# A two-layer hybrid trunk: the triangular inverses of layer 0's delta rule taken two heads at a time, with a new order of projection tiles

## The chip, the cores and the metric

One core of one Trainium2 chip runs the whole program: two layers of a sequence model on 512 tokens (256 latent, 256 context), all weights streamed from HBM. The metric is the time of one execution in microseconds. Before the change it is 1524.98 us, the median of three runs (1524.62 to 1525.18).

## The reference, cut to what matters

Each layer normalizes and modulates its input, projects it once (w_in), runs three branches on column groups of the projection, gates each branch by its own SiLU path, and projects back (w_out) with a gated residual. The change touches one branch, the gated delta rule of four heads, in two directions, in chunks:

```python
strict = jnp.tril(jnp.einsum('bhnid,bhnjd->bhnij', kb, k) * decay, -1)
eye = jnp.eye(cs, dtype=jnp.float32)
t_mat = lax.linalg.triangular_solve(eye + strict, jnp.broadcast_to(eye, strict.shape),
                                    left_side=True, lower=True, unit_diagonal=True)
u = t_mat @ (v * beta[..., None])
w = t_mat @ (kb * jnp.exp(g)[..., None])
...
def step(s, inp):
    q_i, k_i, u_i, w_i, qk_i, gl_i = inp
    v_new = u_i - w_i @ s
    o = q_i @ s + qk_i @ v_new
    s = s * jnp.exp(gl_i)[..., None, None] + jnp.swapaxes(k_i, -1, -2) @ v_new
    return s, o
```

A is `strict`, the strictly triangular matrix of a chunk; its inverse with ones on the diagonal is `t_mat`. The other branches are a linear recurrence (RG-LRU) of four column groups and an attention of eight heads.

## The kernel before

**Tiles and quarters.** A layer's activations lie transposed as 16 blocks of 128 features, each split in a high and a low part, `xh[k]` and `xl[k]`, in a 32-bit format that TensorE multiplies in one pass. A projection tile is 128 output columns; `accumulate` (L399) makes it from three matmuls for each k (`wh` with `xh`, `wl` with `xh`, `wh` with `xl`), 48 in all, into the PSUM tile `pz`. `project` (L405) goes through a tile in four quarters of four k; each quarter needs one pair `wh`, `wl` of 512 columns, which ScalarE (`wh`, a cast) and VectorE (`wl`, the difference) make from the raw weights in `split_w` (L356). There are four such pairs, and `Weights.ahead` (L385) keeps three made ahead. The first seven tiles of layer 0 (`FIRST`, L23) are made during its start; then come 37 tiles in the order of the table `ORDER` (L24) and 16 tiles of w_out. The 37 tiles are called the body here and counted 0 to 36, with quarters as fractions.

**What each tile sets off.** The table's names say whose columns a tile holds: gk, gv, gq are keys, values and queries of a delta-rule head; kc, vc, qc attention; xa the RG-LRU; ga, gb, gc the gates. `consume` (L1097) hands a finished tile to a generator: `gdn_k`, `gdn_v`, `gdn_q`, `attn_...`, `rglru`. `gdn_q` (L750) adds `gdn_head` (L761), one generator for a whole head, to lane 0 of the class `Background` (L470); attention and RG-LRU go to lane 1. Between pairs of k, `between` (L1124) calls `pump`, which issues the next step of each lane whose earlier step should be done by the clocks that `Timed` (L51) keeps while the program is written; where VectorE should be idle it also issues a piece of layer 1's modulation, 512-column multiply-adds into `macc` on VectorE. The build's scheduler then fixes each engine's order. So TensorE's queue is the stream of `pz` matmuls with short stretches of other work between them, and each engine works off its queue in order.

**A head.** `gdn_head` makes the products of k with k and q (`kk`), the decay matrices in two `wa` tiles, and A in a third `wa` tile (`a2`, L785). `invert(a2)` (L872) inverts both directions at once, by blocks: on the diagonal 32x32 blocks four levels of two products (`small`, L897: 16 matmuls of 32x32 each, at 16 places of the array), each followed by work on VectorE (a masked product into `ym`, tile `s`; or an addition and a 32x32 transpose, tiles `tt` and `ti`, both of the tag `c`); then two more such products, and three of 64x64 (`large`, L928: 8 matmuls). That is 13 dependent products a head. The result goes into the tile `full`, of which there is one, and which POOL first clears (L880). Then the head's scan reads it.

**The RG-LRU** (`rglru_scan`, L959) works in a tile `th`, of which there is one. **The end of the body:** after the last tile `bg.drain()` (L1164) issues what is left, and `split_x` (L338) splits the 16 blocks Y of the branches' outputs into `xh[k]` (ScalarE) and `xl[k]` (VectorE) for w_out, whose first tile reads them in the order of k.

Of the kernel before, what the change touches and what calls it, by code (L numbers as in the profile page):

```python
# [13 lines left out]
P = 128  # L14
KT = 16
T = 256
# [8 lines left out]
    "vc0 kc0 gc4 qc0 qc1 gk1 gv1 qc2 gq1 gk2 qc3 gv2 gq2 kc1 vc1 qc4 qc5 gk3 gv3 gc6 qc6 qc7 gb0 gq3 xa0 xa1 gc5 ga2 xa2 gb1 gb2 xa3 gb3 ga0 ga1 ga3 gc7",  # L25
# [69 lines left out]
def trunk(ctx, tc, xT, cT, consts, masks, rope_t, small, fg, w_mod0, w_mod, w_first, w_in, w_ba, w_rg, w_out, out):  # L95
# [121 lines left out]
    class Narrow:  # L217
# [390 lines left out]
    def layer(l, acc, bs):  # L608
# [152 lines left out]
        def gdn_head(h, rq):  # L761
            kq, kt, vt = gd[h]["kq"], gd[h]["kt"], gd[h]["vt"]

            bb = tmp("bb", (P, 2, 4, 2))
            for x, name in enumerate(("beta", "bt")):
                dve.tensor_tensor(out=bb[:, x], in0=gate[name].rearrange("p c (d h) -> p c d h", d=2)[:, :, :, h],
                                  in1=gd[h]["r2"][:, 0:4].unsqueeze(2).to_broadcast([P, 4, 2]), op=ALU.mult)
            kk = [pa_() for _ in range(2)]
            for c in range(4):
                w = 2 * P if c < ncq else P  # L770
                pe.matmul(out=kk[c // 2][:, 256 * (c % 2):256 * (c % 2) + w], lhsT=kq[:, c, 0, :],
                          rhs=kq[:, c].rearrange("p x t -> p (x t)")[:, 0:w], start=True, stop=True)
            kkv = [k_.rearrange("p (c x t) -> p c x t", c=2, x=2) for k_ in kk]
            qkds, dts = [], []
            for d in range(2):
                j = 4 * d + h

                dt_ = tmp("wa")
                nc.sync.dma_start(out=c3(dt_), in_=gate["rd"][:, j, :].partition_broadcast(P))
                pool.tensor_tensor(out=c3(dt_), in0=c3(dt_), in1=maskb[d].unsqueeze(1).to_broadcast([P, 4, P]), op=ALU.add)  # L780
                for c in range(4):
                    act.activation(out=dt_[:, c * P:c * P + P], in_=dt_[:, c * P:c * P + P], func=AF.Exp, bias=gate["ncum"][:, c, j:j + 1])
                dts.append(dt_)
                yield
            a2 = tmp("wa")  # L785
            for c in range(4):
                cc = slice(c * P, c * P + P)
                dve.tensor_scalar(out=a2[:, cc], in0=dts[0][:, cc], scalar1=bb[:, 0, c, 0:1], scalar2=None, op0=ALU.mult)
                dve.scalar_tensor_tensor(out=a2[:, cc], in0=dts[1][:, cc], scalar=bb[:, 0, c, 1:2], in1=a2[:, cc], op0=ALU.mult, op1=ALU.add)
            for x in range(2):  # L790
                dve.tensor_tensor(out=c3(a2[:, 256 * x:], 2), in0=c3(a2[:, 256 * x:], 2), in1=kkv[x][:, :, 0, :], op=ALU.mult)
            yield
            for d in range(2):
                qkd = dts[d]
                for x in range(2):
                    if 2 * x < ncq:
                        dve.tensor_tensor(out=c3(qkd[:, 256 * x:], 2), in0=kkv[x][:, :, 1, :], in1=c3(dts[d][:, 256 * x:], 2), op=ALU.mult)
                qkds.append(qkd)
            yield
            tts = yield from invert(a2)  # L800
# [71 lines left out]
        def invert(a2):  # L872
            rows = [slice(32 * i, 32 * i + 32) for i in range(4)]
            tt = tmp("c", (P, 2, 4, 32))
            ti = tmp("c", (P, 2, 4, 32))
            ac = tmp("s", (P, 4, 32))
            full = tmp("full", (P, 2, TT), bufs=1)
            fv = full.rearrange("p d (c t) -> p d c t", t=P)
            av = c3(a2)
            pool.memset(full, 0.0)  # L880
            for i in range(4):
                (act.copy if i % 2 else dve.tensor_copy)(ac[rows[i]], av[rows[i], :, rows[i]])
            yield
# [401 lines left out]
```

## Time and profile before

| | |
|---|---|
| median of three runs | 1524.98 us |
| the profiled execution | 1525.27 us, span 1523.4 us |
| TensorE (PE) busy | 1466.0 us, 96% of the span |
| VectorE (DVE) busy | 1165.2 us, 76% |
| ScalarE (ACT) busy | 739.3 us, 49% |
| GpSimd (POOL) busy | 110.8 us, 7% |
| layer 0's start | 0 to 143 us |
| layer 0's body, 37 tiles | 143.1 to 731.7 us |
| layer 0's w_out, 16 tiles | 731.7 to about 911 us |
| layer 1 | from about 911 us on |

A matmul's time in a row is from its start to its end, and the next begins before that end; so the time that it costs is read from start to start. In rows of matmuls of plain 32-bit floats the trace has two records for each matmul: "pa<-c,s x32" is one `small` product of 16.

### The profile page before, as it was taken

To read this page: it belongs to the slowest core of one execution; us is meant where nothing else is said; L and a number is where in the kernel's file an instruction comes from. 1 tells how busy PE (TensorE), PEld (TensorE's weight loads), DVE (VectorE), ACT (ScalarE), POOL (GpSimd) and SP (SyncE) were. 2 spreads that over 40 slices of the span, in tenths; PEclk is the share of its full clock that TensorE was granted. 3 is DMA by queue.
4 is the path that set the end of the run, shared out by engine and by line. 5 is a ranking of instruction groups with operands and counts; after the bars stand their busy time and mean duration, and the time that the engine had idled before them with its cause. 6 is when DMAs were issued, how large, how long until landed. Compare 5 with 4: busy or idle time off the path is not lost.

```text
span 1523.4 us, 30014 instructions
## 1 busy us (share of the span) xinstructions
PE 1466.0 (96%) x11762; PEld 1210.7 (79%) x11762; DVE 1165.2 (76%) x2513; ACT 739.3 (49%) x1708; POOL 110.8 (7%) x114
## 2 busy tenths in 40 slices
PE   4999999999999999999999999999999999999996
PEld 3777778777877877788888877778878899779996
DVE  5446898989898798999657877777885776778754
ACT  4324435545444546654422225444544555777653
POOL 0000100100100100000011110010100101000011
PEclk9999999999999999999999999999999999999998
DMA  9994544434443452445346655645542333224653
GB/s 358 396 387 158 163 137 131 145 112 145 154 139 126 129 180 91 132 136 175 125 142 210 217 189 193 186 157 164 190 150 74 98 117 112 71 91 138 192 183 111
DMA packets 87310, 247.68 MB, mean 163 GB/s; under 512 B 9280, under 2 KB 20992, under 8 KB 87168
## 3 DMA queue, kind: packets, MB, share of 16 engines
q1 hardware_dynamic: 86016, 244.71, 48.9%
q8 instruction: 92, 1.51, 0.4%
q10 hardware_dynamic: 1152, 1.05, 0.2%
q14 instruction: 50, 0.41, 0.1%
HBM read 243.60 MB, written 2.13 MB: 161 GB/s over the span
## 4 chain that ended last, share of the span: by engine, by line
PE 76%; DVE 10%; issue 7%; ACT 3%; DMA 2%; POOL 1%; SPq 0%; DVEq 0%; POOLq 0%; ACTq 0%
PE pz L89 55%; PE pa L89 8%; PE pb L89 8%; PE pt L89 3%; PE pm L89 3%; DVE wb L89 2%; DMA wraw<-in_w_in 2%; DVE wl L89 1%; DVE macc L89 1%; DVE th L89 1%; DVE o L89 1%; ACT t L89 1%; ACT wb L89 1%; DVE Y L89 1%; DVE wa L89 1%
## 5 line engine op out<-in xcount | busy, mean ns | idle before, releaser
L89 PE MATMUL pz<-xh,wh 128*128 128x512 f32 (+1 forms) x1760 | 643.8, 366 | 1.8 <-ACT xh L89 1.8
L89 PE MATMUL pz<-xh,wl 128*128 128x512 f32 (+1 forms) x1760 | 629.8, 358 | 0.8 <-DVE wl L89 0.8
L89 PE MATMUL pz<-xl,wh 128*128 128x512 f32 (+1 forms) x1760 | 628.2, 357 | 0.0
L89 ACT CAST wh<-wraw 128x512 fp32r<-128x512 f32 x488 | 294.2, 612 | 339.5 <-PE pz L89 203.3
L89 DVE TENSOR_TENSOR wl<-wraw,wh 128x512 fp32r<-128x512 f32 x488 | 327.6, 679 | 139.4 <-ACT wh L89 137.8
L89 PEld LDWEIGHTS pz<-xl,wh 128*128 128x128 f32 x1760 | 332.1, 189 | 49.4 <-DVE xl L89 0.6
L89 PEld LDWEIGHTS pz<-xh,wh 128*128 128x128 f32 x1760 | 332.1, 189 | 47.5 <-ACT xh L89 1.9
L89 PEld LDWEIGHTS pz<-xh,wl 128*128 128x128 f32 x1760 | 332.7, 189 | 42.7 <-DVE wl L89 1.5
L89 DVE SCALAR_TENSOR_TENSOR macc<-wm,cs,macc 128x512 f32<-128x512 f32 x400 | 293.5, 765 | 1.1 <-DMA wm<-in_w_mod 0.5
L89 PE MATMUL pb<-wb 128*128 128x128 f32 (+1 forms) x560 | 113.4, 330 | 3.9 <-ACT wb L89 2.0
L89 PEld LDWEIGHTS pb<-wb 128*128 128x128 f32 x560 | 80.1, 191 | 17.2 <-ACT wb L89 7.3
L89 POOL TENSOR_TENSOR o<-o,t 128x512 f32<-128x512 f32 (+1 forms) x28 | 30.5, 1091 | 325.7 <-ACT t L89 325.7
L89 ACT ACTIVATE wb<-pb,mx,rqa 128x512 f32<-128x512 f32 (+1 forms) x48 | 33.9, 707 | 41.7 <-DVE mx L89 41.4
L89 DVE SCALAR_TENSOR_TENSOR u<-zp,small,u 128x512 f32<-128x512 f32 (+1 forms) x72 | 50.4, 700 | 2.2 <-ACT u L89 1.9
L89 ACT ACTIVATE t<-pt 128x128 f32<-128x128 f32 (+1 forms) x122 | 34.2, 280 | 32.1 <-PE pt L89 30.1
L89 ACT ACTIVATE xh<-u,modS 128x256 fp32r<-128x256 f32 x64 | 29.3, 502 | 40.7 <-DVE u L89 40.6
L89 DVE TENSOR_SCALAR modA<-pm,nb,small 128x2 f32<-128x2 f32 x16 | 4.5, 278 | 56.8 <-PE pm L89 56.7
L89 PEld LDWEIGHTS pa<-c,s 32*32 32x32 f32 x2304 | 25.1, 107 | 21.8 <-issue 12.2
L89 DVE TENSOR_REDUCE mx<-pb 128x1 f32<-128x512 f32 (+1 forms) x48 | 28.7, 597 | 10.4 <-PE pb L89 10.0
L89 ACT COPY wb<-pb 128x512 f32<-128x512 f32 (+1 forms) x48 | 24.7, 515 | 21.4 <-PE pb L89 20.7
L89 PE MATMUL pa<-c,s 32*32 32x32 f32 x2304 | 33.1, 194 | 1.4 <-DVE c L89 1.2
L89 ACT COPY zp<-pz 128x512 f32<-128x512 f32 (+1 forms) x30 | 17.0, 566 | 34.9 <-PE pz L89 34.7
(264 smaller groups left out, 1774.3 us busy)
## 6 DMA issues: line engine op xcount, KB each, us to landing
wraw<-in_w_in SPq DMA_DIRECT2D x148, 512.0 KB, 3.6
wm<-in_w_mod SPq DMA_DIRECT2D x128, 512.0 KB, 3.7
wraw<-in_w_out SPq DMA_DIRECT2D x64, 512.0 KB, 3.7
wraw<-in_w_first SPq DMA_DIRECT2D x32, 448.0 KB, 5.8
wb<-in_w_mod SPq DMA_DIRECT2D x44, 256.0 KB, 7.0
kq<-in_w_mod SPq DMA_DIRECT2D x10, 512.0 KB, 7.6
Y<-in_xT SPq DMA_DIRECT2D x16, 256.0 KB, 5.1
wa<-rows_d SPq DMA_DIRECT2D x16, 256.0 KB, 5.1
```

What stands on the lines that cost most here:

```text
L89: return f(*args, **kw)
```

## The change

- In layer 0 the heads go in pairs, (0, 1) and (2, 3). `gdn_q` of the odd head adds one generator `gdn_pair` for both, and then `gdn_scan`, the rest of the old `gdn_head`, for each. In layer 1 each head is its own "pair".
- `invert` takes a list of one or two A. `small` and `large` issue the products of both, one after the other, into one PSUM tile; the steps on the other engines follow for both. The second head's `tt`, `ti` and later temporaries lie in the tile `o`.
- A is made in the first half of the tile `full` instead of a `wa` tile, and the inverse is written over it; POOL clears the second half at first, and in the first half what lies outside the blocks, later.
- There are two tiles `full` instead of one `full` and one `th`; the RG-LRU uses them too, and so do the modulation's weights in the start.
- Layer 0's table `ORDER` is new: gk1 gv1 gq1 come first, kc0 and vc0 behind them, gk2 gv2 gq2 directly after gb0, and the tiles gk3 gv3 gq3 together; the xa tiles move from places 24, 25, 28 and 31 to 27, 29, 31 and 33.

```diff
-    "vc0 kc0 gc4 qc0 qc1 gk1 gv1 qc2 gq1 gk2 qc3 gv2 gq2 kc1 vc1 qc4 qc5 gk3 gv3 gc6 qc6 qc7 gb0 gq3 xa0 xa1 gc5 ga2 xa2 gb1 gb2 xa3 gb3 ga0 ga1 ga3 gc7",
+    "gk1 gv1 gq1 vc0 kc0 qc0 qc1 gc4 qc2 gc6 qc3 gb0 gk2 gv2 gq2 kc1 vc1 gk3 gv3 gq3 qc4 qc5 gc5 qc6 ga2 qc7 gb1 xa0 gb2 xa1 gb3 xa2 ga0 xa3 ga1 ga3 gc7",
...
-            bg.add(0, 4 + h, gdn_head(h, rq))
+            gd[h]["rq"] = rq
+
+            hs = (h,) if last else (h - 1, h) if h % 2 else ()
+            if hs:
+                bg.add(0, "pair", gdn_pair(hs))
+            for x in hs:
+                bg.add(0, 4 + x, gdn_scan(x))
+
+
+        def gdn_pair(hs):
+            for h in hs:
...
+                full = tmp("full", (P, 2, TT))
+                a2 = full[:, 0, :]
...
+                pool.memset(full[:, 1, :], 0.0)
                 yield
-            a2 = tmp("wa")
...
+                gd[h].update(bb=bb, qkds=dts, full=full)
+                yield
+            yield from invert([gd[h]["full"] for h in hs])
+
+        def gdn_scan(h):
+            kq, kt, vt, rq, bb, qkds = (gd[h][x] for x in ("kq", "kt", "vt", "rq", "bb", "qkds"))
+            tts = [gd[h]["full"][:, d, :] for d in range(2)]
...
-        def invert(a2):
+        def invert(fulls):
...
-            full = tmp("full", (P, 2, TT), bufs=1)
-            pool.memset(full, 0.0)
+            both = range(len(fulls))
+            o_ = tmp("o") if len(fulls) > 1 else None
+            tt = [four(o_[:, 0:256]) if x else tmp("c", (P, 2, 4, 32)) for x in both]
+            ti = [four(o_[:, 256:512]) if x else tmp("c", (P, 2, 4, 32)) for x in both]
...
                 p = pa_()
-                for c in range(4):
-                    for r in range(4):
-                        u = r ^ across
-                        pe.matmul(out=p[rows[u], 32 * c:32 * c + 32], lhsT=lhsT(r, c, u), rhs=rhs(r, c), start=True, stop=True, tile_position=(32 * r, 32 * u))
-                return p[:, 0:P].rearrange("p (c t) -> p c t", c=4)
+                for x in both:
+                    for c in range(4):
+                        for r in range(4):
+                            u = r ^ across
+                            o = P * x + 32 * c
+                            pe.matmul(out=p[rows[u], o:o + 32], lhsT=lhsT(x, r, c, u), rhs=rhs(x, r, c), start=True, stop=True, tile_position=(32 * r, 32 * u))
+                return [p[:, P * x:P * x + P].rearrange("p (c t) -> p c t", c=4) for x in both]
...
+                for x in both:
+                    hv = mixed(tt[x], slice(0, P), 1, 0, 4, b)
+                    dve.tensor_tensor(out=hv, in0=hv, in1=px[x].rearrange("p c (q x b) -> p (c q) x b", x=2, b=b), op=ALU.add)
+                    dve.transpose(out=flat(ti[x]), in_=flat(tt[x]))
...
+            for x in both:
+                act.activation(out=ym[x], in_=py[x], func=AF.Copy, scale=-1.0)
+                for i in (1, 3):
+                    pool.memset(fv[x][rows[i], 0, :, rows[i - 1]], 0.0)
...
-            th = tmp("th", (P, 2, TT), bufs=1)
+            th = tmp("full", (P, 2, TT))
```

What this moves on the engines is seen at two places. The first is on TensorE, at the start of the first inverse of layer 0. Before, head 0's products stand alone, with six projection matmuls between two of them (`pa<-c,s` is a `small` product; `pz` is the projection):

```order
L89 MATMUL pa<-c,s 32x32 x16
L89 MATMUL pz<-xh_701,wh 128x512
L89 MATMUL pz<-xh_701,wl 128x512
L89 MATMUL pz<-xl_702,wh 128x512
L89 MATMUL pz<-xh_792,wh 128x512
L89 MATMUL pz<-xh_792,wl 128x512
L89 MATMUL pz<-xl_793,wh 128x512
L89 MATMUL pa<-c,s 32x32 x16
```

Now the same products of heads 0 and 1 follow each other (`pa<-o,s` is the second head's), with attention's matmuls behind them (`pb`):

```order
L89 MATMUL pa<-c,s 32x32 x16
L89 MATMUL pa<-o,s 32x32 x16
L89 MATMUL pb<-cst,wb 128x128 x4
L89 MATMUL pz<-xh_701,wh 128x512
L89 MATMUL pz<-xh_701,wl 128x512
L89 MATMUL pz<-xl_702,wh 128x512
L89 MATMUL pz<-xh_792,wh 128x512
L89 MATMUL pz<-xh_792,wl 128x512
L89 MATMUL pz<-xl_793,wh 128x512
L89 MATMUL pa<-c,s 32x32 x16
L89 MATMUL pa<-o,s 32x32 x16
L89 MATMUL pb<-wb 128x128 x4
```

Two products share one entry into the small places of the array, and what lies between two entries is as before.

The second place is on VectorE, at the passage from the body to w_out. Before, the splits of the outputs (`xl<-Y,xh`) alternate with those of the weights (`wl`), and the RG-LRU's last output is long done:

```order
L89 TENSOR_TENSOR wl<-wraw,wh 128x512
L89 SCALAR_TENSOR_TENSOR Y_7998<-t,Y_7998 128x512
L89 TENSOR_TENSOR xl_8096<-Y_6623,xh_8095 128x512
L89 TENSOR_TENSOR xl_8100<-Y_7142,xh_8099 128x512
L89 TENSOR_TENSOR xl_8104<-Y_7015,xh_8103 128x512
L89 TENSOR_TENSOR wl<-wraw,wh 128x512
L89 TENSOR_TENSOR xl_8108<-Y_7998,xh_8107 128x512
L89 TENSOR_TENSOR xl_8112<-Y_3186,xh_8111 128x512
L89 TENSOR_TENSOR xl_8116<-Y_4788,xh_8115 128x512
L89 TENSOR_TENSOR wl<-wraw,wh 128x512
L89 TENSOR_TENSOR xl_8120<-Y_6134,xh_8119 128x512
```

Now the RG-LRU's last sum (`full<-full`), its gated output (`Y_8014`, block 3), the last tile's gate (`t<-t,pz`, `Y_6855`, block 15) and the splits of the outputs stand in one piece (`xl_8113` is the split of block 3), and the next weight splits come behind it:

```order
L89 TENSOR_TENSOR wl<-wraw,wh 128x512
L89 SCALAR_TENSOR_TENSOR full<-wb,full 128x256
L89 TENSOR_TENSOR xl_8105<-Y_7558,xh_8104 128x512
L89 TENSOR_TENSOR full<-full 128x512
L89 TENSOR_TENSOR xl_8109<-Y_6181,xh_8108 128x512
L89 SCALAR_TENSOR_TENSOR Y_8014<-full,Y_8014 128x512
L89 TENSOR_TENSOR xl_8117<-Y_4005,xh_8116 128x512
L89 TENSOR_TENSOR xl_8121<-Y_4543,xh_8120 128x512
L89 SCALAR_TENSOR_TENSOR t<-t,pz 128x512
L89 TENSOR_TENSOR xl_8113<-Y_8014,xh_8112 128x512
L89 SCALAR_TENSOR_TENSOR Y_6855<-t,Y_6855 128x512
```

From here ten more `xl` rows follow (blocks 6 to 15) before the next `wl`, and then four `wl` in a row: 21 instructions from one `wl` to the end of the next, where before at most four others stood between two `wl`.

## Rows read from the trace of the kernel before

**Rows 1.** The page: busy time, share of the span and instructions of each engine.
```profile
PE 1466.0 (96%) x11762; PEld 1210.7 (79%) x11762; DVE 1165.2 (76%) x2513; ACT 739.3 (49%) x1708; POOL 110.8 (7%) x114
```

**Rows 2.** Windows: body, its last 46 us, two tiles of w_out: length, busy time by engine.
```profile
143.10:731.70 588.60, 578.21 (x4284) 457.92 (x4283) 527.96 (x1154) 303.01 (x749) 39.65 (x34) 1.00 0.43 139
685.80:731.70 45.90, 45.90 (x199) 37.25 (x198) 43.90 (x76) 26.70 (x43) 0.00 (x0) 1.00 0.50 166
760.00:782.30 22.30, 22.30 (x98) 18.08 (x97) 7.10 (x12) 6.22 (x11) 2.59 (x2) 1.00 0.36 118
```

**Rows 3.** Waits of PE in the body: us in total, times, longest.
```profile
PE pt L89 <- ACT t L89: 1.7, 1, 1.7
PE pt L89 <- DVE wb L89: 1.3, 1, 1.3
...
PE pt L89 <- DVE kv L89: 0.6, 1, 0.6
```

**Rows 4.** Timeline of PE, a small product between projection matmuls: start us, us, instruction.
```profile
206.11 0.40 PE L89 MATMUL pz<-xl,wh 128*128 128x512 f32 x1
206.44 0.45 PE L89 MATMUL pa<-c,s 32*32 32x32 f32 x32
206.82 0.50 PE L89 MATMUL pz<-xh,wh 128*128 128x512 f32 x1
207.16 0.39 PE L89 MATMUL pz<-xh,wl 128*128 128x512 f32 x1
```

**Rows 5.** Timeline of PE, a small product in two pieces, between other work.
```profile
1129.48 0.31 PE L89 MATMUL pa<-c,s 32*32 32x32 f32 x10
1129.72 0.66 PE L89 MATMUL pt<-cst,kq 128*128 128x128 f32 x4
1130.31 0.38 PE L89 MATMUL pa<-c,s 32*32 32x32 f32 x22
1130.62 0.50 PE L89 MATMUL pz<-xh,wh 128*128 128x512 f32 x1
```

**Rows 6.** Timeline of PE, a large product in two pieces.
```profile
368.85 0.33 PE L89 MATMUL pa<-full,c 64*64 64x64 f32 x4
369.11 0.66 PE L89 MATMUL pt<-cst,kq 128*128 128x128 f32 x4
369.70 0.56 PE L89 MATMUL pa<-full,c 64*64 64x64 f32 x12
370.19 0.50 PE L89 MATMUL pz<-xh,wl 128*128 128x512 f32 x1
```

**Rows 7.** Timeline of PE, a small product with attention's work behind it.
```profile
453.95 0.46 PE L89 MATMUL pa<-c,s 32*32 32x32 f32 x32
454.34 0.44 PE L89 MATMUL pb<-cst,wb 128*128 128x128 f32 x2
```

**Rows 8.** Timeline of DVE: modulation, splits of the outputs and of the weights.
```profile
636.69 1.41 DVE L89 SCALAR_TENSOR_TENSOR macc<-wm,cs,macc 128x512 f32<-128x512 f32 x2
...
728.03 2.49 DVE L89 TENSOR_TENSOR xl<-Y,xh 128x512 fp32r<-128x512 f32 x4
730.44 0.69 DVE L89 TENSOR_TENSOR wl<-wraw,wh 128x512 fp32r<-128x512 f32 x1
```

**Rows 9.** DVE in the body by form: count, busy, mean ns, idle before.
```profile
L89 DVE STREAM_TRANSPOSE c<-c 128x256 f32<-128x256 f32 x20 | 8.7, 435 | 0.1
...
L89 DVE TENSOR_TENSOR c<-c,pa 128x128 f32<-128x128 f32 x16 | 4.5, 281 | 4.4 <-PE pa L89 4.4
```

**Rows 10.** Timeline of ACT, then DVE, at w_out's start: how far weights are made ahead.
```profile
743.08 0.62 ACT L89 CAST wh<-wraw 128x512 fp32r<-128x512 f32 x1 [2.13 <-PE pz L89]
...
746.56 0.69 DVE L89 TENSOR_TENSOR wl<-wraw,wh 128x512 fp32r<-128x512 f32 x1 [2.00 <-ACT wh L89]
```

**Rows 11.** Timeline of PE and DVE: the last RG-LRU group to its sum.
```profile
694.80 0.85 PE L89 MATMUL pb<-wb 128*128 128x512 f32 x3
...
710.91 0.69 DVE L89 TENSOR_TENSOR Y<-th 128x512 f32<-128x512 f32 x1
```

More of the change, by code (lines that the diff above doesn't have):

```diff
@@ L914, in invert @@
[L914 to L924 removed]
+                px = small(lambda x, r, c, u: ym[x][rows[r], c, :], lambda x, r, c: mixed(tt[x], rows[r], 1, c, 1, b), 0)
@@ L925, in invert @@
+            yield
+            px = small(lambda x, r, c, u: ym[x][rows[r], c, :], lambda x, r, c: tt[x][rows[r], 1 - r % 2, c, :], 1)
+            for x in both:
+                for i in range(4):
+                    copy = act.copy if i % 2 else dve.tensor_copy
+                    copy(fv[x][rows[i], :, :, rows[i]], tt[x][rows[i]])
+                    copy(fv[x][rows[i], i % 2, :, rows[i ^ 1]], px[x][rows[i]])
             yield
@@ L930, in large @@
                 p = pa_()
-                for c in range(4):
-                    for r in range(2):
-                        u = r ^ across
-                        pe.matmul(out=p[half[u], 64 * c:64 * c + 64], lhsT=lhsT(r, c, u), rhs=rhs(r, c), start=True, stop=True, tile_position=(64 * r, 64 * u))
-                return p[:, 0:T].rearrange("p (c t) -> p c t", c=4)
-            pt = large(lambda r, c, u: fv[half[r], r, c, half[r]], lambda r, c: ident[half[r], half[r]], 0)
-            t2 = tmp("c", (P, 4, 64))
@@ L939, in invert @@
-            act.copy(out=t2, in_=pt)
-            yield
-            py = large(lambda r, c, u: av[half[r], c, half[u]], lambda r, c: t2[half[r], c, :], 1)
-            y2 = tmp("c", (P, 4, 64))
-            act.activation(out=y2, in_=py, func=AF.Copy, scale=-1.0)
+                for x in both:
+                    for c in range(4):
+                        for r in range(2):
+                            u = r ^ across
+                            o = T * x + 64 * c
+                            pe.matmul(out=p[half[u], o:o + 64], lhsT=lhsT(x, r, c, u), rhs=rhs(x, r, c), start=True, stop=True, tile_position=(64 * r, 64 * u))
@@ L944, in invert @@
+            y2 = [wide4(o_[:, 256:512]) if x else tmp("c", (P, 4, 64)) for x in both]
+            for x in both:
+                act.activation(out=y2[x], in_=py[x], func=AF.Copy, scale=-1.0)
+                pool.memset(fv[x][half[1], 0, :, half[0]], 0.0)
             yield
-            px = large(lambda r, c, u: y2[half[r], c, :], lambda r, c: fv[half[r], 1 - r, c, half[r]], 1)
-            for u in range(2):
-                (act.copy if u else dve.tensor_copy)(fv[half[u], u, :, half[1 - u]], px[half[u]])
+            px = large(lambda x, r, c, u: y2[x][half[r], c, :], lambda x, r, c: fv[x][half[r], 1 - r, c, half[r]], 1)
@@ L948, in invert @@
+            for x in both:
+                for u in range(2):
+                    (act.copy if u else dve.tensor_copy)(fv[x][half[u], u, :, half[1 - u]], px[x][half[u]])
             yield
-            return [full[:, d, :] for d in range(2)]
         def rglru(t, pz):
```

122 lines of the change are left out of this document (58 added, 64 removed).

## The prediction

> **What bounds the kernel now.** I read the page first. TensorE is busy for 96% of the span, VectorE for 76%, GpSimd hardly [rows 1]. So time comes off only where TensorE's own queue gets shorter or a wait of TensorE goes. The windows come next: in layer 0's body, where nearly the whole change lies, TensorE is idle for 588.60 - 578.21 = 10.4 us, and VectorE is busy for 527.96 of 588.60 us; in the last 46 us TensorE has no idle time and VectorE 2 us in 46 [rows 2]. VectorE is thus the engine to watch: it makes `wl` for every quarter tile, in the same queue as all that the heads need. The waits then say which idle time this change could touch: three waits for `pt`, where keys, values and queries are transposed in the first tiles, with 1.7 + 1.3 + 0.6 = 3.6 us [rows 3]. The rest are short waits of attention and of the scans, which the change leaves alone. Last the timeline of single products, since the change takes away no matmul: it only sets two runs side by side.
>
> I work on the profiled execution, 1525.27 us; the median shown is 0.3 us below it.
>
> **Common runs.** A projection matmul takes 0.23 us from start to start (98 records in the 22.30 us of two tiles, of which two are cut at the edges) [rows 2]. An isolated small product delays the stream by 207.16 - 206.11 - 2 x 0.23 = 0.59 us: from a projection start to the second one behind the product, less the two projection steps in it [rows 4]. What does a second product of 16 cost in the same run? The trace has products in pieces: 10 records (5 matmuls) take 0.24 us to the next start and 22 records 0.31 [rows 5]. So 12 more records cost 0.07, and 32 more by that slope 0.19; the whole product between other work, where no projection neighbour pays for the change of shape, takes 454.34 - 453.95 = 0.39 [rows 7], which as the price of a second run is the upper bound, a saving of 0.59 - 0.39 = 0.20. I take 0.23, as in the middle of the slope and the piece of 10, so an isolated product saves 0.59 - 0.23 = 0.36, and one that had other work beside it 0.39 - 0.23 = 0.16. For large products 4 records take 0.26 and 12 take 0.49 [rows 6]: 0.029 a record, so 8 more matmuls cost 16 x 0.029 = 0.46 and the fixed part, saved by a merge, is 0.15 beside other work and some 0.35 alone.
>
> How many merges there are, the order of the two programs says: 26 (two pairs of 13 products). But TensorE's stretches between projection matmuls go only from 231 to 219, because new breaks arise elsewhere: the first products of pair and scan, and attention's, no longer fall together so often. So 12 of the 26 save the full 0.36 (4.3 us), 14 save the neighbour's 0.2 (2.8), and some five runs more of other work cost 0.17 each (0.9): **-6.2 us**. The bounds are 26 x 0.15 = -3.9 and 26 x 0.36 = -9.4.
>
> The Trainium skill (TensorEngine Tiling (Array Packing), Key Properties) says that a change of tiling mode drains TensorE. By that every merge takes away one full drain whatever stands beside it, and the sum here would be the lower bound's side, about -9. The small product beside attention's matmuls at 0.39 instead of 0.59 [rows 4, 7] speaks against so even a price.
>
> **The start.** With gk1 gv1 gq1 first, the transposes that wait for 3.6 us now have 15, 7, 15 and 21 projection matmuls between them instead of 9, 5, 10 and 4 in the order. Some of the waits go, others come with the tighter row of delta-rule tiles: **-1.5 us**, within 0 and -3.6.
>
> **The scans' end and layer 1.** The scan of head 1 now follows that of head 0 at once, so one transposition of the output waits a little longer: +0.6. Layer 1's heads are single as before; its stretches go from 189 to 191, its own runs down by three: -0.6. Together nothing, within 1 us either way. POOL's additional clearing hides at 7% of the span [rows 1]; the second buffer `full` takes a wait from the RG-LRU that no row shows TensorE to pay.
>
> **VectorE's queue.** Here the new order costs. Weights are made three quarters ahead: at w_out's start ACT waits 2.13 us for TensorE to free a buffer before it makes `wh`, in 0.62, and VectorE follows with `wl` in 0.69 [rows 10]. A quarter of bare projection is 12 x 0.23 = 2.8 us, so the lead of `wl` is at most 3 x 2.8 - 0.62 - 0.69 = 7.1 us, more where the quarters hold other work. Steps of VectorE of 512 columns follow each other at 0.62 (four splits in 2.49), multiply-adds into `macc` at 0.70 [rows 8]. Two places exceed that lead.
>
> At tiles 32 to 34, where xa2, xa3 and the gates now come together, VectorE has from the `wl` of quarter 32.0 to that of 34.75 in the new order 76 instructions: 20 into `macc` (14.0), 11 `wl` and 26 others of 512 columns (37 x 0.62 = 22.9) and 19 shorter (at 0.4 on average, between 0.28 and 0.62 [rows 8, 9]: 7.6), in sum 44.5 us. TensorE needs for these 11 quarters 11 x 2.8 and 3.4 of other work, 34.1. The lead before is 8.7 (three quarters with 1.6 us of other work in them), so 44.5 - 34.1 - 8.7 = 1.7 us stay; with a lead of 7.1 it is 3.3. I take **+2.1 us** (0 to 3.3).
>
> At the body's end 21 instructions stand from one `wl` to the next: 21 x 0.60 = 12.6 us against a lead of 7.1 and one quarter, 9.9: about 2.7, and with a `t` row that waits for ACT **+2.9 us** (0 to 6). Before, the same splits alternated with `wl` [rows 8] and nothing stalled. In the same row hangs block 3: before, the last RG-LRU group went from its product at 694.80 to its sum at 710.91 [rows 11], 16 us, with 36 us to w_out to hide in; now 54 projection matmuls, 12.5 us, lie between that product and w_out's first, and `xl` of block 3 is needed 11 matmuls later, at 15 us. The 16 us become 16 instead of 36 covered; the missing 1 us lies inside the 2.9.
>
> **Sum:** -6.2 - 1.5 + 0 + 2.1 + 2.9 = -2.7 us: 1522.6 for the profiled execution, **1522.3 us** on the scale of the median.
>
> **Rivals.**
> - *VectorE keeps up.* The scheduler put `wl` late because its clocks saw time for it, and the row of 21 starts earlier than I think, since Y's of the early blocks are long done: the lags cost 1 us instead of 5.0. For it: in the last 46 us before VectorE is as full [rows 2] and TensorE doesn't wait. Against: the sums of durations above. Time: 1525.0 - 6.2 - 1.5 + 1 = 1518.3; with the bound of -9.4 for the merges it is 1515.
> - *The end of the body breaks (slower).* One mechanism: the last xa tile now at place 33 puts the RG-LRU's chain, the gates and 16 splits into one queue of VectorE right before w_out. Its own sixteen steps on VectorE take some 10 us of the 16 [rows 8, 11]; the rest is other rows in the queue. Should as many rows again stand before the chain, it ends 6 us later, and the queue behind it with it: 6 us more than the 5.0 counted. Then 1525.0 - 6.2 - 1.5 + 11 = 1528.3. It decides from 8 us of lag on. For it: VectorE's 44 of 46 us [rows 2]; against: `macc` is issued only where VectorE should be idle.
> - *The pair's chain holds TensorE up (slower).* Each hop gets longer by the second head's step, 0.28 for a masked product, 0.28 + 0.44 for the addition and the transpose [rows 9], while six projection matmuls, 1.4 us, and attention's lie between two products as before. Should 0.35 a hop show on 20 hops, that is 7 us: 1525.0 - 2.7 + 7 = 1529.3. Against: none of the 13 products waits in the rows of waits above, and `pump` issues a step when it should be ready.
> - *No common runs.* If the scheduler parted the pairs, -6.2 would go and 1528.5 stay. One of 21 small runs is parted in the order, so this has no weight.
>
> **How the numbers follow.** The forecast 0.48, VectorE keeps up 0.27, the end breaks 0.15, the chain holds 0.10. The forecast's own range is 1518 to 1526 (bounds of the merges +2.3 and -3.2, of the start +1.5 and -2.1, of the lags). What a measurement here can tell from no change is 0.2%, 3 us. Of the forecast's 0.48 half lies below 1522; with nearly all of the second case that is 0.49 faster; the rest of the forecast and part of the slow cases lie within 0.2% (1522 to 1528), 0.34; slower are 0.17. The range goes to 1515 below, the second case with every merge at its upper bound, and to 1530 above, beyond both slow cases.
>
> **What would show it.** Common runs: rows "pa<-c,s" with "pa<-o,s" behind them, 0.2 to 0.25 us from the second's start to the next, and TensorE's busy time some 6 us less. The lags: waits of TensorE for `wl` about 2 us near tile 34 and about 3 at w_out's start, none before; waits for `xl` there say that block 3 is the late one. The start: waits for `pt` between 0 and 3.6 us. The chain: waits of `pa` for `c`, `s` or `o` over 2 us in the whole body would show the third rival. The forecast is wrong in its reason, even with the right time, if TensorE's busy time falls by less than 4 us or if no wait for `wl` or `xl` appears.

## The result: slower by 0.7%, and the profile after

The changed kernel takes 1536.17 us (median; 1532.65 to 1539.08), against 1524.85 for the kernel before, timed beside it: ratio 1.0067, interval 1.0047 to 1.0087. The forecast was 1522.3, in a range that ended at 1530. The profiled execution is 1535.12 us, its span 1533.3 against 1523.4.

The page after, its row of busy time [rows 1]:

```profile
PE 1463.7 (95%) x11762; PEld 1211.0 (79%) x11762; DVE 1159.4 (76%) x2516; ACT 735.2 (48%) x1701; POOL 115.6 (8%) x138
```

TensorE was busy for less and the span grew, so the time went into waits. The windows after, with the columns of [rows 2]: tiles 0 to 3, the whole body, tiles 32 to 36, and w_out.

```profile
144.60:209.80 65.20, 61.11 (x269) 45.56 (x268) 58.42 (x127) 33.81 (x99) 10.98 (x9) 0.95 0.48 154
144.60:737.60 593.00, 576.29 (x4301) 459.89 (x4299) 527.95 (x1157) 296.57 (x737) 43.09 (x46) 0.99 0.44 141
671.60:737.60 66.00, 63.49 (x286) 49.95 (x284) 65.06 (x109) 43.13 (x67) 0.53 (x1) 1.00 0.41 136
737.60:936.00 198.40, 194.89 (x989) 155.11 (x988) 127.77 (x212) 55.05 (x94) 20.75 (x15) 0.98 0.53 174
```

Column by column: the body is 4.4 us longer than in [rows 2], TensorE's idle time there is 593.00 - 576.29 = 16.7 us instead of 10.4, and the granted clock (third from the end) is no longer 1.00, above all in tiles 0 to 3 (0.95). TensorE's waits in the body after [rows 3]:

```profile
PE pb L89 <- DVE wb L89: 4.3, 8, 0.8
PE pt L89 <- ACT t L89: 4.1, 2, 3.6
PE pz L89 <- DVE wl L89: 2.0, 1, 2.0
PE pt L89 <- DVE kq L89: 1.8, 1, 1.8
```

Every stretch of a profile can be divided in three: TensorE's idle time; what the lower clock cost (busy time times one minus the granted clock, summed over windows of 1 us); and the rest, called work here. For both kernels, each profiled twice (the second time as e9 and e17; w_out runs here to the first projection matmul of layer 1, at 926.3 us before, and so takes in the passage between the layers):

| us | before | again | after | again |
|---|---|---|---|---|
| start, length | 143.1 | 144.2 | 144.6 | 143.6 |
| body, length | 588.6 | 589.0 | 593.0 | 595.0 |
| body: idle, tiles 0 to 3 | 3.6 | 2.9 | 4.1 | 4.7 |
| body: idle, tiles 4 to 31 | 6.8 | 7.2 | 10.1 | 11.0 |
| body: idle, tiles 32 to 36 | 0.0 | 0.0 | 2.5 | 2.5 |
| body: lost to the clock | 0.0 | 0.0 | 2.7 | 3.4 |
| w_out, length | 194.5 | 193.3 | 198.4 | 198.9 |
| w_out: idle | 1.3 | 1.6 | 3.5 | 3.5 |
| w_out: lost to the clock | 1.7 | 0.0 | 3.4 | 3.4 |
| layer 1, length | 597.2 | 594.8 | 597.3 | 597.2 |
| whole program: work | 1457.3 | 1458.6 | 1452.6 | 1452.8 |

The means of each pair differ by 0.5 (start), 5.2 (body), 4.8 (w_out) and 1.3 us (layer 1), together 11.7, and the medians by 11.3. The start and layer 1 are within what one kernel differs from itself (1.1 and 2.4 us). Of the clock's 3.4 us in the body the second time, 1.7 are lost in tiles 0 to 3 and 1.7 behind a wait at tile 34; in w_out the clock is lost in the passage between the layers.

**The wait at the start.** Of the waits forecast to shrink, the three of [rows 3] became one of 3.63 us, with one of 0.46 ahead of it. TensorE's timeline after:

```profile
182.66 0.40 PE L89 MATMUL pz<-xl,wh 128*128 128x512 f32 x1
186.68 1.12 PE L89 MATMUL pt<-cst,kq 128*128 128x128 f32 x4 [3.63 <-ACT t L89]
187.45 0.78 PE L89 MATMUL pz<-xh,wh 128*128 128x512 f32 x1
188.03 0.63 PE L89 MATMUL pz<-xh,wl 128*128 128x512 f32 x1
```

After the wait a projection matmul takes 0.43 us from start to start instead of 0.23. The windows show why (granted clock third from the end):

```profile
186.68:192.20 5.52, 5.52 (x15) 4.53 (x16) 5.52 (x10) 4.46 (x17) 3.00 (x3) 0.51 0.02 4
192.20:198.00 5.80, 5.80 (x28) 4.72 (x27) 4.71 (x10) 4.11 (x11) 1.73 (x2) 1.00 0.51 182
```

0.51 is 1.2 GHz, 1.00 is 2.4 GHz. ScalarE's timeline says who was late: three exponentials of `wa` stand ahead of the copies of the first transposes (`t<-pt`) and wait 4.78 us for GpSimd.

```profile
177.09 0.62 ACT L89 CAST wh<-wraw 128x512 fp32r<-128x512 f32 x1 [0.98 <-PE pz L89]
182.49 0.99 ACT L89 ACTIVATE wa<-wa,ncum 128x128 f32<-128x128 f32 x3 [4.78 <-POOL wa L89]
183.39 0.56 ACT L89 COPY zp<-pz 128x512 f32<-128x512 f32 x1
183.85 0.27 ACT L89 ACTIVATE t<-pt 128x128 f32<-128x128 f32 x1
```

In the kernel before, too, exponentials stand ahead of such copies, but they wait 1.73 us:

```profile
181.36 0.40 ACT L89 ACTIVATE wa<-wa,ncum 128x128 f32<-128x128 f32 x1 [1.73 <-POOL wa L89]
```

GpSimd's timeline after shows what it waited for: the rows of decays, fetched back from HBM, to which it adds the mask.

```profile
181.24 1.22 POOL L89 TENSOR_TENSOR wa<-wa,msk 128x512 f32<-128x512 f32 x1 [3.85 <-DMA wa<-rows_d]
183.36 1.15 POOL L89 TENSOR_TENSOR wa<-wa,msk 128x512 f32<-128x512 f32 x1 [0.90 <-DMA wa<-rows_d]
```

**The end of the body.** The two lags of VectorE came. TensorE's timeline after, first in tile 34, then at w_out's start:

```profile
709.04 0.50 PE L89 MATMUL pz<-xh,wl 128*128 128x512 f32 x1 [2.01 <-DVE wl L89]
...
740.76 0.50 PE L89 MATMUL pz<-xh,wh 128*128 128x512 f32 x1 [0.79 <-ACT xh L89]
742.48 0.51 PE L89 MATMUL pz<-xl,wh 128*128 128x512 f32 x1 [0.99 <-DVE xl L89]
749.70 0.50 PE L89 MATMUL pz<-xh,wl 128*128 128x512 f32 x1 [0.67 <-DVE wl L89]
```

The first two of w_out's waits fall on the tenth and the twelfth matmul of its first tile, which are block 3's: 1.78 us for block 3, and 0.67 for `wl`. VectorE's timeline shows the block of splits that stands ahead of the weights, where [rows 8] had four:

```profile
742.93 6.11 DVE L89 TENSOR_TENSOR xl<-Y,xh 128x512 fp32r<-128x512 f32 x10
748.95 2.50 DVE L89 TENSOR_TENSOR wl<-wraw,wh 128x512 fp32r<-128x512 f32 x4
```

### The profile page after: what moved, and what is told of

The parts are those of the page before. It is cut to its first block, busy times and chain, and to the rows that moved or that the text cites. A ratio compares the mean times of both kernels' runs of the same rounds, so it can differ in the third digit from the quotient of the medians.

```text
span 1533.3 us, 30027 instructions
## 1 busy us (share of the span) xinstructions
PE 1463.7 (95%) x11762; PEld 1211.0 (79%) x11762; DVE 1159.4 (76%) x2516; ACT 735.2 (48%) x1701; POOL 115.6 (8%) x138
## 4 chain that ended last, share of the span: by engine, by line
PE 75%; DVE 13%; DMA 4%; ACT 4%; issue 2%; POOL 1%; SPq 0%; DVEq 0%; ACTq 0%; POOLq 0%
PE pz L89 51%; PE pa L89 9%; PE pb L89 8%; PE pt L89 4%; PE pm L89 3%; DVE wb L89 2%; DVE wl L89 2%; DVE full L89 2%; DVE macc L89 2%; DMA wa<-rows_d 1%; DMA wm<-in_w_mod 1%; DVE o L89 1%; DVE u L89 1%; ACT wb L89 1%; DVE xl L89 1%
## 5 line engine op out<-in xcount | busy, mean ns | idle before, releaser
L89 ACT ACTIVATE s<-pa,bb 128x128 f32<-128x128 f32 x96 | 29.1, 368 | 15.1 <-PE pa L89 15.0
L89 DVE TENSOR_REDUCE mx<-pb 128x1 f32<-128x512 f32 (+1 forms) x48 | 28.6, 595 | 10.2 <-PE pb L89 10.1
L89 POOL MEMSET full<- 32x128 f32 (+2 forms) x32 | 10.3, 322 | 335.7 <-PE pa L89 184.3
L89 PE MATMUL pb<-cst,wb 128*128 128x128 f32 x160 | 27.2, 279 | 7.7 <-DVE wb L89 6.9
```

The source lines that it names most:

```text
L89: return f(*args, **kw)
```

## The experiments

**e1 and e2: the two halves of the change.** e1 is the kernel before with the new line of `ORDER`, e2 the changed kernel with the old one:

```diff
-    "vc0 kc0 gc4 qc0 qc1 gk1 gv1 qc2 gq1 ...
+    "gk1 gv1 gq1 vc0 kc0 qc0 qc1 gc4 qc2 ...
```

> The kernel before with the new tile order alone: no pairs, no common runs. Theory (the order costs through VectorE's queue at tiles 33 to 35 and at w_out's start, about 4.5 us together, and through the start): 1529 to 1533 us, with waits of TensorE for wl or xl at both places. Rival (the longer chain of the pair is what costs, the order is harmless): 1524 to 1526 us.

> The changed kernel with the old tile order: pairs and common runs alone. Theory (common runs save about 5 us of TensorE's busy time, and the longer chain shows in few waits): 1519 to 1523 us. Rival (the longer chain of the pair holds TensorE up): 1529 us or more, with waits of pa for c, s or o over 4 us in the body.

e1: 1539.12 us, ratio 1.0090 (1.0077 to 1.0103). e2: 1540.70, 1.0102 (1.0088 to 1.0116). By the medians each half costs more than the whole (e1's interval overlaps the whole's 1.0047 to 1.0087), so the costs don't add. e1 is above its expectation. e2 went to the rival by its time, but not by its sign: with the old order TensorE waits in the body for `pa` 6.4 us, of which 2.7 for `o` and 0.7 for `s` are the 3.4 that the rival wanted over 4, and 3.0 are one wait for `wa` before the second pair's first product; that pair's work crowds into tiles 28 to 36 there. e1's work is 1461.3 us, 4.0 more than before, with 245 stretches of other work between projection matmuls in layer 0 instead of 231: 0.29 us a stretch (0.19 against the second profile of the kernel before). e2 has 248 stretches; its work is 1456.8. By the price of 0.29 the 17 stretches more cost 4.9, so by this estimate common runs save 5.4 there. In both, TensorE waits at the start in one piece (3.8 and 3.5 us) and the clock costs 3.0 and 1.7 us in tiles 0 to 3; in both, exponentials in ScalarE's queue had waited for GpSimd's mask before that (6.48 and 4.30 us). So either half alone brings that wait.

**e3: the pair without common runs.**

```diff
-            yield from invert([gd[h]["full"] for h in hs])
+            for h in hs:
+                yield from invert([gd[h]["full"]])
```

> The changed kernel with the pair's two inverses one after the other, each product alone: what common runs are worth with all else the same. Theory (they save about 5 us): 1540 to 1543 us, TensorE's busy time in layer 0's body 4 to 6 us higher than in the changed kernel. Rival (common runs save nothing, since TensorE changes shape anyway): 1535 to 1538 us.

1551.13 us, 1.0169 (1.0154 to 1.0183), above both expectations. The work is 1461.3 us, 8.7 more than after; TensorE's busy time in the body is 13.4 higher, part of it at the lower clock, and its idle time 5.0. So the pair's products cost more apart; but 24 more stretches are in it (243 against 219), 7 us at e1's price, and what a common run saves can't be read from it.

**e8: a third set of products in each small run.**

```diff
+                if len(fulls) > 1:
+                    for c in range(4):
+                        for r in range(4):
+                            u = r ^ across
+                            o = 2 * P + 32 * c
+                            pe.matmul(out=p[rows[u], o:o + 32], lhsT=lhsT(1, r, c, u), rhs=rhs(1, r, c), start=True, stop=True, tile_position=(32 * r, 32 * u))
```

> The changed kernel with a third set of 16 small products in each of the 20 small runs of layer 0's pairs (a copy of the second head's into an unused part of the PSUM tile, read by nobody): what 16 more matmuls cost in a common run. Theory (0.23 us each): TensorE's busy time without the loss to the clock rises by 4 to 5.5 us. Rival (a set costs 0.39 us or more, as between other work, and merging saves only 0.2): 7.5 us or more.

The total went to the rival (work 1460.2, 7.6 us more), but the order around the runs moved too, so the price is read from the rows. TensorE's timeline, first after:

```profile
256.04 0.45 PE L89 MATMUL pa<-c,s 32*32 32x32 f32 x32 [0.97 <-DVE s L89]
256.32 0.48 PE L89 MATMUL pa<-o,s 32*32 32x32 f32 x32
256.73 1.16 PE L89 MATMUL pb<-wb 128*128 128x128 f32 x8
```

and in e8:

```profile
256.17 0.45 PE L89 MATMUL pa<-c,s 32*32 32x32 f32 x32 [0.97 <-DVE s L89]
256.44 0.74 PE L89 MATMUL pa<-o,s 32*32 32x32 f32 x64
257.11 1.16 PE L89 MATMUL pb<-wb 128*128 128x128 f32 x8
```

From start to start the first set costs 0.28, the last 0.41, one more between them 0.67 - 0.41 = 0.26. Twenty of them are 5.2 us, as the theory had it; where the other 2.4 come from isn't shown. So a run of two with other work behind it costs 0.69, while two single products there cost 2 x 0.39 [rows 7]. Among projection matmuls a run of two stands after at

```profile
261.86 0.40 PE L89 MATMUL pz<-xl,wh 128*128 128x512 f32 x1
262.19 0.45 PE L89 MATMUL pa<-c,s 32*32 32x32 f32 x32
262.46 0.48 PE L89 MATMUL pa<-o,s 32*32 32x32 f32 x32
...
263.21 0.39 PE L89 MATMUL pz<-xh,wl 128*128 128x512 f32 x1
```

It delays the stream by 263.21 - 261.86 - 2 x 0.23 = 0.89 us, while two isolated products cost 2 x 0.59 [rows 4].

**e4: the exponentials held.** They take their bias from a copy of `ncum` that needs the norms of head 1's keys.

```diff
+            zz = tmp("mx", (P, 4))[:, 0:1]
+            dve.tensor_scalar(out=zz, in0=gd[hs[-1]]["r2"][:, 0:1], scalar1=0.0, scalar2=None, op0=ALU.mult)
+            nc2 = tmp("spe", (P, 32), bufs=1).rearrange("p (c j) -> p c j", j=8)
+            dve.tensor_scalar(out=nc2, in0=gate["ncum"], scalar1=zz, scalar2=None, op0=ALU.add)
...
-                        act.activation(out=dt_[:, c * P:c * P + P], in_=dt_[:, c * P:c * P + P], func=AF.Exp, bias=gate["ncum"][:, c, j:j + 1])
+                        act.activation(out=dt_[:, c * P:c * P + P], in_=dt_[:, c * P:c * P + P], func=AF.Exp, bias=nc2[:, c, j:j + 1])
```

> The changed kernel with the pair's exponentials (wa on ScalarE) made to need the norms of head 1's keys, so that they can't stand in ScalarE's queue ahead of the copies of the first transposes while their rows are still under way from HBM. Theory (that queue costs a wait of 3.6 us and then 11 matmuls at the lower clock, some 2.3 us): 1529 to 1532 us, no wait over 2 us before tile 3, granted clock 1.00 from 180 to 200 us, and runs closer together than the 6 us of the changed kernel. Rival (the rows are late for TensorE anyway, and the wait goes elsewhere): 1535 to 1537 us.

1534.87 us, 1.0070 (1.0052 to 1.0089): just below the rival's range, and the wait went elsewhere, as the rival had it. It moved from ScalarE's copies to VectorE's values of gv1 and grew to 4.49 us. VectorE's timeline shows a cause that I had not on the list:

```profile
180.78 0.68 DVE L89 SCALAR_TENSOR_TENSOR kq<-t,u 128x512 f32<-128x512 f32 x1
181.38 1.66 DVE L89 SCALAR_TENSOR_TENSOR u<-zp,small,u 128x512 f32<-128x512 f32 x1
182.97 1.65 DVE L89 TENSOR_TENSOR wl<-wraw,wh 128x512 fp32r<-128x512 f32 x1
184.54 1.13 DVE L89 TENSOR_SCALAR rq<-rq 128x4 f32<-128x4 f32 x1
185.59 1.73 DVE L89 SCALAR_TENSOR_TENSOR u<-zp,small,u 128x512 f32<-128x512 f32 x1
187.23 0.74 DVE L89 SCALAR_TENSOR_TENSOR macc<-wm,cs,macc 128x512 f32<-128x512 f32 x1
```

Steps of 0.7 us take 1.65, and one of 0.15 takes 1.13 (`rq`), as long as GpSimd adds masks:

```profile
180.59 1.91 POOL L89 TENSOR_TENSOR wa<-wa,msk 128x512 f32<-128x512 f32 x1 [3.77 <-DMA wa<-rows_d]
182.66 4.10 POOL L89 TENSOR_TENSOR wa<-wa,msk 128x512 f32<-128x512 f32 x3 [0.17 <-DMA wa<-rows_d]
```

The Trainium skill has the rule (GPSIMD Engine Reference, Specifications): GpSimd shares its SBUF interfaces with VectorE and contends with VectorE's instructions that have two SBUF inputs or run in a 2-port mode. These rows agree for the steps with two inputs (`u`, `wl`): 0.9 to 1.0 us for each that is slowed, nearly a mask's own 1.2; in which mode `rq`, with one, ran no row tells. Nor is every step slowed: `kq` at 180.78 kept its 0.68, and the mask beside it took 1.91 instead of 1.2. The kernel before has such steps too (a step into `macc` at 182.1 us took 1.70), so the change doesn't bring them; it is their place that differs.

**e5, e6, e7: other places in the table.** e5 puts gk1 gv1 gq1 behind vc0 kc0; e6 puts qc4 and qc5 between gk3, gv3 and gq3; e7 draws the xa tiles two places forward.

```diff
-gk1 gv1 gq1 vc0 kc0 qc0 ...
+vc0 kc0 gk1 gv1 gq1 qc0 ...
-... gk3 gv3 gq3 qc4 qc5 ...
+... gk3 qc4 gv3 qc5 gq3 ...
-... qc4 qc5 gc5 qc6 ga2 qc7 gb1 xa0 gb2 xa1 gb3 xa2 ga0 xa3 ga1 ...
+... qc4 qc5 qc6 qc7 gc5 xa0 ga2 xa1 gb1 xa2 gb2 xa3 gb3 ga0 ga1 ...
```

> The changed kernel with gk1 gv1 gq1 behind vc0 and kc0 instead of ahead of them, the rest of the order as changed. Theory (the three delta-rule tiles at the very start crowd the transposes into one wait of 3.6 us, which also costs the clock 2.7): no wait over 2 us and granted clock 1.00 in tiles 0 to 4, 1530 to 1533 us. Rival (a wait of that size belongs to the start whatever the order, since the decay rows are late): the wait stays at 3 us or more, 1535 to 1537 us.

> The changed kernel with qc4 and qc5 between gk3, gv3 and gq3, which stand together in the change. Theory (three delta-rule tiles in a row crowd the transposes there as at the start: waits of 1.8 and 0.8 us at 446 to 462 us): these two waits go, idle time of tiles 12 to 19 falls from 5.2 to 3 us, 1533 to 1535 us. Rival (the waits there come from the pair's chain, not from the row of tiles): idle time of 5 us in these tiles remains.

> The changed kernel with attention's last tiles drawn together and the xa tiles at places 25, 27, 29 and 31 instead of 27, 29, 31 and 33. Theory (the late RG-LRU groups crowd VectorE's queue): no idle time of TensorE in tiles 32 to 36 and about 1 us in w_out instead of 2.5 and 3.5, 1530 to 1533 us; its 7 more stretches between projection matmuls take back 2 us of that. Rival (the crowding moves with the xa tiles): the same 4 to 6 us of idle time earlier, in tiles 25 to 32, 1536 to 1540 us.

e5: 1537.95 us (1.0092, 1.0074 to 1.0110). e6: 1546.03 (1.0136, 1.0116 to 1.0155). e7: 1541.57 (1.0108, 1.0090 to 1.0126). None of the three theories held, and the rivals are right in kind. In e5 the wait stays (2.87 us, clock 3.0); in e6 4.5 us of idle time stay in tiles 12 to 19, and 10.2 arise in tiles 32 to 36; in e7 w_out's idle time falls to 1.5 us, but 6.7 us stand in tiles 32 to 36, nearly all of them in tile 32, two tiles ahead of the lag of the changed kernel, as the xa tiles are. No place for these tiles was the cause alone.

**e10: no filler at the end.**

```diff
-HOLD = 2
+HOLD = 7
```

> The changed kernel with the modulation's pieces kept out of the last seven tiles of the body instead of the last two (24 of their steps fall to other places, some to TensorE). Theory (VectorE's crowded queue makes wl late, and the filler is a third of that queue): idle time of tiles 32 to 36 falls from 2.5 to under 0.5 us, that of w_out from 3.5 to about 2.5; TensorE's work grows by 1 to 2 us; 1532 to 1536 us. Rival (the RG-LRU's own steps make wl late): 2 us of idle time in tiles 32 to 36 remain.

1546.39 us, 1.0138 (1.0121 to 1.0155). Tiles 32 to 36 have 1.6 us of idle time instead of 2.5 (one wait for `wl` of 0.99 instead of 2.01), between the theory's 0.5 and the rival's 2, so the filler made about half of that lag. What it leaves undone comes in the passage between the layers, and w_out grows by 9.7 us, so the time is far above the expected.

**e12 and e11: the masks out of GpSimd.** e12 leaves GpSimd's addition out, and its exponentials take another bias and multiply the rows by 0, though they still wait for them; e11 is e4 with the addition on VectorE, by this edit:

```diff
-                    pool.tensor_tensor(out=c3(dt_), in0=c3(dt_), in1=maskb[d].unsqueeze(1).to_broadcast([P, 4, P]), op=ALU.add)
+                    dve.tensor_tensor(out=c3(dt_), in0=c3(dt_), in1=maskb[d].unsqueeze(1).to_broadcast([P, 4, P]), op=ALU.add)
```

> The changed kernel without the addition of the masks to wa (the decay matrices are wrong: the exponentials take another bias and leave the rows out), so GpSimd does nothing between the rows' arrival and the exponentials. Theory (rows, mask and exponentials in one chain hold ScalarE's queue, and GpSimd's 1.2 us per mask is a part of it): the wait before the second transposes falls from 3.6 to about 2.4 us. Rival (the rows' arrival alone decides): 3.3 us or more.

> The kernel of e4_hold with the masks added to wa on VectorE instead of GpSimd. Theory (in e4_hold four of these additions ran on GpSimd while VectorE made the first values, and VectorE's 0.7 us steps beside them took 1.65, so that the transposes of gv1 waited 4.5 us): no stretched step of VectorE, idle time in tiles 0 to 3 falls from 4.9 to 3 us or less and the clock's loss there to 0; 1530 to 1534 us. Rival (VectorE, in order, now itself waits for the rows from HBM): idle time of 4 us or more.

e12, one run: 1526.13 us; the wait is 2.68 us, nearer to the theory than to the rival, and the clock still loses 1.6 us behind it; idle time in tiles 12 to 19 is 2.5 instead of 5.2. ScalarE's timeline there: the exponentials stand where they stood, and wait for the rows alone.

```profile
180.11 1.28 ACT L89 ACTIVATE wa<-wa,neg 128x128 f32<-128x128 f32 x4 [3.54 <-DMA wa<-rows_d]
```

So about 1 us of the wait of 3.63 is the mask's, and the rest comes with the rows and the queue. e11: 1523.35, 0.9989 (0.9976 to 1.0001): 13 us less than the changed kernel and below its expectation, though not clear of the kernel before. Idle time of tiles 0 to 3 is 1.1 us and the clock stays up.

**e13 and e14: the edit shown above alone, in either kernel.**

> The changed kernel with the masks added to wa on VectorE, the exponentials not held. Theory (GpSimd's mask and its stretching of VectorE's steps are the cost, and ScalarE's queue follows from it): 1522 to 1527 us, idle time of tiles 0 to 3 under 2.5 us. Rival (ScalarE's queue behind the exponentials is the cost, which the rows from HBM set): a wait of 2.7 us or more at the second transposes stays, with 1.5 us or more lost to the clock, 1526 to 1532 us.

> The kernel before with the masks added to wa on VectorE. Theory (there the masks come one head at a time and cost little; 8 more stretches between projection matmuls in each layer cost 2 us each): 1526 to 1532 us. Rival (the masks on GpSimd cost any kernel of this form some 8 us): 1515 to 1520 us.

e13: 1522.44 us, 0.9982 (0.9969 to 0.9994), as expected. e14: 1520.09, 0.9963 (0.9949 to 0.9977), at the rival's edge. Thus the edit is worth 13.7 us by the medians in the changed kernel (13.0 by the ratios) and 5.0 (5.6) in the kernel before: 7 to 9 us of the change's 10 to 11 go with the place of the masks. Windows of e13 (tiles 0 to 3, the body, tiles 12 to 19):

```profile
145.34:205.21 59.87, 58.74 (x269) 43.56 (x267) 56.86 (x124) 31.32 (x90) 5.86 (x5) 1.00 0.51 168
145.34:730.59 585.25, 575.45 (x4300) 457.69 (x4299) 525.12 (x1161) 296.76 (x738) 31.90 (x38) 1.00 0.44 142
340.75:458.40 117.65, 114.99 (x609) 92.80 (x608) 107.31 (x230) 57.90 (x159) 7.40 (x7) 1.00 0.50 162
```

and the body of e14:

```profile
144.23:734.32 590.09, 582.60 (x4300) 459.36 (x4299) 533.63 (x1174) 304.13 (x749) 31.40 (x26) 1.00 0.44 141
```

In the changed kernel the edit shortens the body by 7.8 us (593.0 to 585.3); in the kernel before it doesn't (588.6 to 590.1). But it changes more than the engine: the scheduler now puts the first mask and its exponentials behind the copies that had stood behind them. Timelines of ScalarE and VectorE in e13:

```profile
180.91 0.28 ACT L89 ACTIVATE t<-pt 128x128 f32<-128x128 f32 x1
...
195.38 1.28 ACT L89 ACTIVATE wa<-wa,ncum 128x128 f32<-128x128 f32 x4
...
194.62 0.69 DVE L89 TENSOR_TENSOR wa<-wa,msk 128x512 f32<-128x512 f32 x1
```

So e13, like e11, takes away the blocked queue and VectorE's slowed steps at once, and its expectation's two causes are not told apart by it: e4 shows that freeing the queue alone is not enough, e12 that dropping the mask alone leaves 2.68 us.

Between e13 and e14 the body gets shorter by the change, 585.3 against 590.1 us. That is given back in w_out (3.9 us idle against 1.3) and in parts that the profiles don't repeat; by the medians e13 stays 2.3 us behind e14, with overlapping intervals. e14 is by the medians the fastest kernel of the study, e13 the one that has the change and still beats the kernel before.

**e15, e16: both edits of e11 with other orders.** e15 takes the old table, e16 the xa tiles one place earlier each.

> The kernel of e11 (masks on VectorE, exponentials held) with the old tile order. Theory (with the masks out of the way the new order gains by its fewer stretches, 216 against 238): 1529 to 1535 us. Rival (the new order costs by itself): 1516 to 1521 us.

> The kernel of e11 with the xa tiles one place earlier each (places 26, 28, 30 and 32). Theory (the late RG-LRU groups crowd VectorE's queue at the end of the body): idle time of tiles 32 to 36 and w_out together falls from 6.4 to 4 us or less, 1520 to 1522 us. Rival (the crowding moves with them): 6 us or more remain, 1523 to 1527 us.

e15: 1539.73 us, 1.0090 (1.0077 to 1.0104), above the theory's 1529 to 1535 and still further from the rival: pairs need the new order, but not for the fewer stretches that the theory named. Work is only 1.3 us above e11's, while the body's idle time is 21.8 us instead of 10.4 and its clock loses 5.9 instead of nothing. e16: 1526.69, 1.0007 (0.9998 to 1.0015): 6.3 us of idle time in tiles 32 to 36 and w_out remain of 6.4, as the rival had it.

**e9 and e17: both kernels once more**, in the table above.

> The kernel before, profiled once more, to see how far the parts of a profile repeat. If the differences between the two kernels' parts are due to the change, busy time without the clock's loss and the idle time of each stretch of the body repeat within 1 us; the program's start (19.8 us idle before, 21.2 after) may differ by 1.5 us by chance, since its instructions up to the first matmul are the same.

> The changed kernel, profiled once more. If its waits are the change's: a wait of 3 to 4 us before the second transposes with 1.5 to 3 us lost to the clock behind it, idle time of 4.5 to 5.5 us in tiles 12 to 19, 2 to 3 us in tiles 32 to 36 and 3 to 4 us in w_out, as in its first profile. What the clock loses at w_out's end and in layer 1 (6.7 us in the first) is chance and may come out anywhere from 2 to 9 us.

The idle time of layer 0's body and w_out comes back to 0.9 us in each row, and the wait at the start is 3.74 us. The work of the kernel before differs by 1.3 us, a little more than expected. What the clock loses at the passage between the layers and in layer 1 doesn't come back (7.0 us in the first profile of the kernel before, 1.7 in the second).

## Why the prediction was wrong, step by step

- **The start, -1.5: the step that failed.** I counted projection matmuls between the transposes and let the three waits of [rows 3] shrink with their number. The late one was not TensorE's spacing: rows from HBM, GpSimd's mask and ScalarE's exponentials are one chain, and in the new order of ScalarE's queue three exponentials stand ahead of the copies that TensorE needs. One wait of 3.63 us came in the place of three, and the clock then cost 2.7 us (1.7 the second time): +3.2 instead of -1.5. With the exponentials held this wait went, and one of 4.49 came by VectorE's slowed steps (e4); with the masks on VectorE as well, tiles 0 to 3 have 1.1 us of idle time and lose nothing to the clock (e11, e13). The order of ScalarE's queue was there to read; I read TensorE's and VectorE's.
- **POOL: its clearing was weighed, its masks were not.** I let POOL's additional clearing hide at 7% of the span; no run tests that. The masks on the same engine were no term at all, and the share says nothing of who waits for them or whom they slow. e13 against the changed kernel gives 13.7 us for eight masks a layer, moved to VectorE and later in the queues, 7 to 9 of them more than in the kernel before; e4 shows 0.9 to 1.0 us lost by a step of VectorE that a mask slows.
- **Common runs, -6.2: right in kind, too large.** Work fell by 4.7 us (5.8 in the second pair of profiles). The second set takes 0.41 us to the next start and not the 0.2 to 0.25 that was to show it; the slope of 22 records against 10 [rows 5] was too flat a price. A merged isolated product saves 2 x 0.59 - 0.89 = 0.29 instead of 0.36; one beside other work 2 x 0.39 - 0.69 = 0.09 instead of 0.2 (for which my own working had 0.16). 12 x 0.29 + 14 x 0.09 = 4.7, or 3.8 after taking off the 0.9 for five runs more, with the prices of small products used for the large ones too. That was an error of 1.5 us and not the cause. TensorE's busy time fell by 2.3 us only, less than the 4 that I had set as a sign of a wrong reason, since the lower clock took back 2.4 over the whole program.
- **Scans and pairs in tiles 4 to 31, 0: wrong by 3.3 us.** Idle time there grew from 6.8 to 10.1 us. 2.5 of it, in tiles 12 to 19, go with the masks of heads 2 and 3 (2.5 us before, 5.2 after, 2.7 in e13). The hops of the pair show in two waits of `pa` for `s`, 1.5 us together: the third rival is small.
- **VectorE's lag at tile 34, +2.1: right** (2.5 us idle in the last five tiles, one wait for `wl` of 2.01). **At w_out's start, +2.9: right in sum, not in its parts.** The three waits there are 2.45 us, before none; but 1.78 of them are block 3's, which I had at 1, and `wl` took 0.67. Over w_out idle time grew by 2.0 to 2.2 us.
- **The clock was no term of my sum.** [rows 2] show it at 1.00 throughout the body, and I let a wait cost only its length. It cost 2.7 to 3.4 us in the body. In the passage at w_out's end it cost 1.7 to 3.4 more, but whether that belongs to the change isn't shown: e11 and e13 lose nothing there, and e14, without the change, loses 3.4.

The sum with the measured terms: -4.7 + 0.5 and 2.7 (start and its clock) + 3.3 + 2.5 + 2.2 + 1.7 (clock in w_out) = 8.2, of the 9.9 between the first two profiles; the other 1.7 are the program's start, 1.4 longer, where the kernel before differs from itself by 1.1, and roundings. Neither slower rival is what happened: the end of the body had 4.7 us of lags and not 11, the pair's chain 1.5 and not 7.

Not settled: e13's edit also changes the order on every engine (layer 1 has 181 stretches instead of 191), so its 13.7 us aren't the masks' price alone, and 3.8 us of the difference of the profiles lie in layer 1, which has no pairs; in the body, tiles 0 to 3 and 12 to 19 account for 5.3 and 2.8 of the 7.8 that it is shorter. How the start's wait divides between the queue and the slowed steps stays open.

## What to carry to other kernels

When a change draws two chains together, follow each of their links to the first thing that waits for a transfer, on every engine's queue, the 7% engine's too: an in-order queue that has one early instruction with a late input holds up all behind it (here ScalarE's, for 4.78 us). Price a wait of TensorE above its length where it falls together with others into one, for the clock may fall behind it (2.7 us behind one of 3.63 here). And read busy time, idle time and clock apart: here a true saving of 5 us of work stood beside 11 to 12 us of new idle time, and the repair lay in neither half of the change.

## What the runs showed of the hardware

- Beside GpSimd's additions of 128x512 (1.15 to 1.2 us each undisturbed), VectorE's steps took up to 1.0 us longer (e4: 0.68 to 1.65 for `wl`); one step kept its time, and the addition took 1.91 us.
- Three waits of 0.6, 1.7 and 1.3 us within 14 us cost the clock nothing; one of 3.63 did (granted 0.51 for the 5.5 us after it). Of the 13 profiles with one wait of 2.68 to 4.49 us in tiles 0 to 3, 12 lost 1.5 to 3.0 us to the clock there and one (e15, 3.45 us) nothing; of the six with none over 2 us, one lost 1.6 (e14) and five nothing.
- A product of 16 matmuls of 32x32 among projection matmuls delayed the stream by 0.59 us, and two of them in one run by 0.89.
- Two profiles of the kernel before differed by 5.4 us in what the clock cost over the whole program, with the idle time of each part of layer 0's body and w_out alike to 0.7 us.
